# A hybrid decoder layer: the up projection of seven chunks by Strassen's seven block products

## The chip, the cores and the metric

The kernel runs on one core of one Trainium2 chip. The metric is the device time of one execution in microseconds, median of several runs. TensorE (PE) multiplies, VectorE (DVE) and ScalarE (ACT) do elementwise work, GpSimd (POOL) little, and SyncE (SP) issues the DMAs. Each engine works through its own queue in order; semaphores tie the queues together.

## The reference

One decoder layer over 256 tokens of width 2048, all in float32:

```python
h = rmsnorm(x, mix_pre_gain)
q_a, k_a, v_a, q_r, f_r, i_r, g_r = split(h @ w_in)          # w_in: 2048 x 5376
m = concat[rmsnorm(sliding_window_attention(q_a, k_a, v_a, sinks)), hgrn2(q_r, f_r, i_r, g_r)]
x = x + rmsnorm(m @ w_out, mix_post_gain)                     # w_out: 2048 x 2048
h = rmsnorm(x, mlp_pre_gain)
u = relu(h @ w_up)                                            # w_up: 2048 x 8192
x = x + rmsnorm((u * u) @ w_down, mlp_post_gain)              # w_down: 8192 x 2048
```

Most of the arithmetic lies in the two projections of the last block, `w_up` and `w_down`.

## The kernel before

**Numbers.** Every operand of a large product is split in two float32r parts: `hi`, the value cast by ACT (line 84 for weights), and `lo`, the value less `hi`, by DVE (line 85). A product is three matmuls, hi x hi, hi x lo and lo x hi (`three`, lines 103 to 107).

**Two forms of product.** The *token-major* form (`wide_step`) holds 128 tokens of the activations in PE and streams 512 weight columns; its result has tokens on the partitions. The *feature-major* form (`feature_step`, lines 113 to 120) holds 128 weight columns and streams the activations: `hi` and `lo` of 256 tokens side by side, 512 columns, against the weight's `hi`, and 256 columns against its `lo`. The two halves of the result stand in one PSUM bank, and `unit_sum` adds them: ACT copies one half, DVE adds the other (lines 140 and 141). A unit (`unit_feature`) is 256 output features: two banks of 16 steps each. Its result has features on the partitions, as the down projection needs it.

**Phases.** First the normalised `x` is transposed, and `w_in` is applied: keys and values, four units for attention (`attention`), and for each of four pairs of recurrent heads two units and one token-major pair (`rnn_pair`). Then `w_out`, token-major, in four column groups of 512. Then the feed-forward part, in four chunks of 2048 features of `w_up`. The first chunk begins with 512 features token-major (they can start while the second 128 tokens are still being normalised); everything else of `w_up` is done in feature-major units, 30 of them. A unit's result is scaled, clipped and squared (`up_evac`), split in `hi` and `lo`, and written to a tile `uT`. After each chunk's up projection stand its 16 down tile rows: four column groups `c` of 512, for each 16 steps on both token blocks. Column groups 0 to 2 are added into `y` by DVE after every chunk; group 3 stays in two PSUM banks to the end.

**Buffers and order.** Weights pass through one pool `wpool` that lives for the whole kernel: three raw tiles of 128x2048 (one megabyte in HBM each), four `hi` and four `lo`. PSUM has three banks named `pj`, three `sc`, one `o`, one `tr`. The order on PE is written out by hand from the last `w_out` group to the first feature unit; everywhere else, and for the other engines and SP throughout, a scheduler sets it from the program's dependences when the kernel is built. A DMA waits in SP's queue until its buffer is free, and so do all DMAs behind it.

**Names and lines** that the change touches: `load_raw`, `split_weight`, `load_unit`, `load_wide`, `load_pair` (70 to 101), `feature_step` and `unit_feature` (113 to 135), `unit_sum` (137), the evacuations in `attention` and `rnn_pair`, the residual and its transposes (`residual` 612, `turn` 619, which writes the transposed `hi` and `lo` in lines 625 and 631), `early_turn` and `up_evac` (662 to 680), and the chunk loop (753 to 773). `mu0` to `mu3`, `hT0` to `hT3` are tags of tiles for activations.

## Time and profile before

| | us |
|---|---|
| median of 3 runs | 1134.54 |
| lowest, highest | 1132.27, 1135.0 |
| profiled execution | 1136.72 |
| its span, first to last instruction | 1134.7 |
| PE busy | 1113.9 |
| DVE busy | 642.8 |
| ACT busy | 554.4 |
| chain of work that ended last, share of PE | 95% |
| bytes read from HBM, mean rate | 201.36 MB, 179 GB/s |

The phases in the span: `w_in` and the heads to 346 us, `w_out` from 321 (its first products lie among the last of the heads) to 414, the feed-forward part from 414 to 1125, the last normalisation to the end. Busy time of PE counts overlapping matmuls once, and the ends of matmuls are modelled; how long one occupies PE is read from the distance between the starts of two. A line "A <- B: total, times, longest" in the list of waits says how long A's engine stood idle until B released it.

### The profile page before, as it was taken

What the parts mean: (1) busy time and instruction counts of PE and PEld (TensorE: products, weight loads), DVE (VectorE), ACT (ScalarE), POOL (GpSimd) and SP (SyncE); (2) the same over time, 40 slices, a digit from 0 to 9 for tenths busy, and PEclk for the clock granted to TensorE, in tenths of its full rate; (3) what the DMA queues carried; (4) which work ended last, traced back from release to release, by engine and by line L of the source; (5) the groups of instructions that cost most, each with busy time, mean ns of one, the idle gap of its engine ahead of it and who ended that gap; (6) DMA issues with size and microseconds to landing.
All of it is one profiled execution on the core that took longest, in us unless ns stands there. A gap on an engine that the chain in (4) does not pass through costs nothing.

```text
span 1134.7 us, 14265 instructions
## 1 busy us (share of the span) xinstructions
PE 1113.9 (98%) x5822; PEld 945.9 (83%) x5822; DVE 642.8 (57%) x728; ACT 554.4 (49%) x747; POOL 25.6 (2%) x56
## 2 busy tenths in 40 slices
PE   8998999999999999999999999999999999999996
PEld 7887788888888888888888888888888888888885
DVE  6755577666655585564445555444655544465453
ACT  6655656645554466553444544334554334454441
POOL 2100001000000010000000000000000000000001
PEclk9999999999999999999999999999999999999998
DMA  8753244444457655746565565555555555655542
GB/s 270 234 165 112 75 148 149 149 148 151 147 196 280 202 197 163 223 162 209 194 198 185 165 211 197 185 189 183 190 182 203 203 188 170 201 177 196 194 139 74
DMA packets 155251, 204.38 MB, mean 180 GB/s; under 512 B 3833, under 2 KB 110898, under 8 KB 154674
## 3 DMA queue, kind: packets, MB, share of 16 engines
q1 hardware_dynamic: 155186, 203.48, 55.0%
q8 instruction: 45, 0.74, 0.3%
q14 instruction: 20, 0.16, 0.0%
HBM read 201.36 MB, written 2.10 MB: 179 GB/s over the span
## 4 chain that ended last, share of the span: by engine, by line
PE 95%; DVE 2%; ACT 0%; issue 0%; POOL 0%; DVEq 0%; ACTq 0%; POOLq 0%
PE pj L118 18%; PE sc L118 10%; PE pj L105 8%; PE pj L106 8%; PE pj L107 8%; PE pj L117 8%; PE sc L107 5%; PE sc L106 5%; PE sc L105 5%; PE sc L117 5%; PE tr L106 1%; PE o L106 1%; PE tr L107 1%; PE o L105 1%; PE tr L105 1%; PE o L107 1%
## 5 line engine op out<-in xcount | busy, mean ns | idle before, releaser
L85 DVE TENSOR_TENSOR wlo<-raw,whi 128x2048 fp32r<-128x2048 f32 (+2 forms) x204 | 427.7, 2102 | 358.2 <-ACT whi L84 357.8
L84 ACT CAST whi<-raw 128x2048 fp32r<-128x2048 f32 (+2 forms) x204 | 357.6, 1760 | 310.7 <-PE sc L107 87.0
L118 PE MATMUL pj<-hT,whi 128*128 128x512 f32 x864 | 309.6, 402 | 3.6 <-DVE qT L141 2.2
L117 PE MATMUL pj<-hT,wlo 128*128 128x256 f32 x810 | 229.7, 284 | 0.4 <-DVE wlo L85 0.3
L118 PEld LDWEIGHTS pj<-hT,whi 128*128 128x128 f32 x864 | 161.7, 190 | 38.3 <-DVE qT L141 2.7
L118 PE MATMUL sc<-hT,whi 128*128 128x512 f32 x480 | 170.0, 398 | 0.0
L117 PEld LDWEIGHTS pj<-hT,wlo 128*128 128x128 f32 x810 | 154.3, 191 | 3.9 <-DVE wlo L85 1.0
L117 PE MATMUL sc<-hT,wlo 128*128 128x256 f32 x450 | 126.6, 281 | 0.0
L118 PEld LDWEIGHTS sc<-hT,whi 128*128 128x128 f32 x480 | 89.3, 188 | 19.7
L105 PE MATMUL pj<-whi,mu 128*128 128x512 f32 x256 | 100.1, 392 | 0.4 <-DVE mg L607 0.4
L106 PE MATMUL pj<-wlo,mu 128*128 128x512 f32 x256 | 99.8, 390 | 0.0
L105 PE MATMUL sc<-whi,mu 128*128 128x512 f32 x256 | 99.6, 389 | 0.0
L106 PE MATMUL sc<-wlo,mu 128*128 128x512 f32 x256 | 99.6, 389 | 0.0
L107 PE MATMUL sc<-whi,mu 128*128 128x512 f32 x256 | 99.6, 389 | 0.0
L107 PE MATMUL pj<-whi,mu 128*128 128x512 f32 x256 | 99.5, 391 | 0.0
L117 PEld LDWEIGHTS sc<-hT,wlo 128*128 128x128 f32 x450 | 85.1, 189 | 1.2
L105 PE MATMUL pj<-whi,hT 128*128 128x512 f32 x160 | 63.9, 402 | 1.1 <-DVE zq L141 1.0
L106 PE MATMUL pj<-wlo,hT 128*128 128x512 f32 x160 | 63.9, 400 | 0.0
L107 PE MATMUL pj<-whi,hT 128*128 128x512 f32 x160 | 63.7, 399 | 0.0
L105 PEld LDWEIGHTS pj<-whi,mu 128*128 128x128 f32 x256 | 48.1, 188 | 10.5 <-DVE mg L607 0.8
L107 PEld LDWEIGHTS pj<-whi,mu 128*128 128x128 f32 x256 | 48.1, 188 | 10.0
L106 PEld LDWEIGHTS sc<-wlo,mu 128*128 128x128 f32 x256 | 48.0, 188 | 10.0
(248 smaller groups left out, 1224.5 us busy)
## 6 DMA issues: line engine op xcount, KB each, us to landing
raw<-in_w_up_dram SPq DMA_DIRECT2D x64, 1024.0 KB, 5.4
raw<-in_w_down_dram SPq DMA_DIRECT2D x64, 1024.0 KB, 5.0
raw<-in_w_in_dram SPq DMA_DIRECT2D x24, 1024.0 KB, 5.4
raw<-in_w_in_dram SPq DMA_DIRECT2D x35, 512.0 KB, 4.1
raw<-in_w_out_dram SPq DMA_DIRECT2D x16, 1024.0 KB, 5.0
xb<-in_x_dram SPq DMA_DIRECT2D x8, 256.0 KB, 6.3
x<-in_x_dram SPq DMA_DIRECT2D x2, 1024.0 KB, 10.5
out_dram<-x SPq DMA_DIRECT2D x6, 256.0 KB, 2.6
```

The costliest lines, as they stand in the source:

```text
L84: nc.scalar.copy(out=hi[:, k], in_=raw[:, k])
L85: nc.vector.tensor_tensor(out=lo[:, k], in0=raw[:, k], in1=hi[:, k].bitcast(F32), op=ALU.subtract)
L105: nc.tensor.matmul(o, lhsT=ah, rhs=bh, start=first, stop=False)
L106: nc.tensor.matmul(o, lhsT=ah, rhs=bl, start=False, stop=False)
L107: nc.tensor.matmul(o, lhsT=al, rhs=bh, start=False, stop=last)
L117: nc.tensor.matmul(ps[:, 0:S], lhsT=al, rhs=both[:, 0, :], start=False, stop=False)
L118: nc.tensor.matmul(ps, lhsT=ah, rhs=both, start=kt == 0, stop=kt == NKT - 1)
```

## The change

The up projection of the last 7168 features is made of seven chunks of 1024. Each chunk is a 256 x 2048 by 2048 x 1024 product, cut in 2 x 2 blocks: tokens in two halves of 128, the depth in two halves of 1024, the features in two halves of 512. Strassen's scheme makes the four result blocks from seven block products instead of eight, at the price of sums of blocks. All products are token-major, three matmuls for each of eight depth steps; a product is made in two halves of 12 matmuls.

- The sums of activation blocks are made once, before the first of the seven chunks, and kept as `hi` and `lo` (`a11`, `s1` to `s4`, `a12`, `a22`). For them `turn` writes the transposed activations a third time, in float32 (`hf`).
- The sums of weight blocks are made by DVE in place for each chunk, on the raw tiles `X`, `P`, `Q` (`add`), between the splits: 8 additions of 128x2048, and 14 splits instead of 8.
- The result blocks are made by accumulating products in PSUM where the signs allow, otherwise by DVE with intermediate results in `scr` and in the unused quarter of `y`. Because they are token-major, every 128x512 block is transposed on PE (`turn_u`) before the down projection, four turns for each chunk; the turns of a chunk stand among the next chunk's first products.
- The chunk loop interleaves: after every product of chunk `ch` stands one half (4 depth steps on both token blocks) of a down tile of chunk `ch - 1`. The order on PE is written out by hand to the end.
- The first 1024 features are done token-major without Strassen's scheme.
- In the first phase a feature unit now makes three 256-wide matmuls for each step into one half of a single bank, so that `unit_sum` goes away: one DVE operation scales and evacuates the unit. The query is scaled there, and the distance penalty of attention no longer passes through ACT.
- The weight pool is entered three times instead of once: `wpool_a` to the end of the heads, `wpool_b` to the start of the chunks, `wpool_c` behind that, with three `hi`, three `lo` and two each of `X`, `P`, `Q` and `d` (down weights). The residual `x2` is written to HBM and read again at the end.

The diff, cut to its core:

```diff
-    wpool = ctx.enter_context(tc.tile_pool(name="wpool", bufs=4))
+    pool_w = tc.tile_pool(name="wpool_a", bufs=4, side="right")
+    wp = [pool_w.__enter__()]
...
     def feature_step(ps, ch, hT, ct, kt):
...
+        three(ps[:, ct * 256:(ct + 1) * 256], [t[:, kt % 8, ct * P:(ct + 1) * P] for t in ch[kt // 8]],
+              [hT[kt // 4][:, kt % 4, i, :] for i in range(2)], kt == 0, kt == NKT - 1)
...
-        qT = unit_sum(apool, "t2", ps_q, 3, "qT")
+        qT = apool.tile([P, 2, S], F32, tag="t2", name=nm("qT"), bufs=3)
+        nc.vector.tensor_tensor(out=qT, in0=ps_q, in1=rb, op=ALU.mult)
...
     pa.__exit__(None, None, None)
-    bpool = ctx.enter_context(tc.tile_pool(name="phase_b", bufs=1))
+    pool_w.__exit__(None, None, None)
+    keep = ctx.enter_context(tc.tile_pool(name="keep", bufs=1, side="right", reuse_waits="tile"))
+    upool = ctx.enter_context(tc.tile_pool(name="upool", bufs=1, side="right", reuse_waits="tile"))
+    pool_w = tc.tile_pool(name="wpool_b", bufs=4, side="right", reuse_waits="tile")
+    wp[0] = pool_w.__enter__()
+    pb = tc.tile_pool(name="phase_b", bufs=1, reuse_waits="tile")
...
+        nc.sync.dma_start(out=x2_dram[tb], in_=x2[tb])
+        hf[tb] = keep.tile([P, NKT, P], F32, tag=f"acc{tb}", name=nm("hf"))
...
+        for i in range(4):
+            kt = 4 * c + i
+            nc.scalar.activation(out=hf[tb][:, kt, :], in_=ps[:, i * P:(i + 1) * P], func=AF.Copy,
+                                 scale=g_mlp[:, kt:kt + 1])
...
+    def turn_u(uT, cb, tb, u, tag, bufs):
+        tp = bank(tag, bufs)
         for i in range(4):
+            nc.tensor.transpose(tp[:, i * P:(i + 1) * P], u[:, i * P:(i + 1) * P], ident)
+        u2 = upool.tile([P, 4, P], F32, tag="u2", name=nm("u2"), bufs=2)
         nc.scalar.activation(out=u2, in_=tp.rearrange("p (a t) -> p a t", a=4), func=AF.Square)
+        hi, lo = (uT[cb][:, :, i, tb * P:(tb + 1) * P] for i in range(2))
         nc.scalar.copy(out=hi, in_=u2)
         nc.vector.tensor_tensor(out=lo, in0=u2, in1=hi.bitcast(F32), op=ALU.subtract)
...
+    nc.vector.tensor_sub(out=tmp, in0=hn[1, 0], in1=hn[1, 1])
+    a11 = split_act(hn[0, 0], "ex")
+    s1 = split_act(tmp, "mu2")
...
+    def product(o, aT, w, h, fresh):
+        for j in range(4):
+            kt = 4 * h + j
+            (ah, al), (bh, bl) = (aT[:, kt, 0, :], aT[:, kt, 1, :]), (w[0][:, j, :], w[1][:, j, :])
+            for i, (a, b) in enumerate(((ah, bh), (ah, bl), (al, bh))):
+                nc.tensor.matmul(o, lhsT=a, rhs=b, start=fresh and kt == 0 and i == 0, stop=kt == 7 and i == 2,
+                                 skip_group_check=not fresh)
...
+    for ch in range(1, NCH):
...
+        for h in range(2):
+            if ch > 1 or h == 1:
+                next_turn()
+            X.append(raw_tile("X", w_up_v, 4 * h, f0))
+            product(bank_a, a11, split_weight(None, X[h], bufs=3), h, True)
+        nc.scalar.copy(out=sv, in_=bank_a)
+        for h in range(2):
+            next_turn()
+            Pq.append(raw_tile("P", w_up_v, 4 * h, f0 + 512))
+            add(X[h], Pq[h])
+            product(bank_b, s1, split_weight(None, X[h], bufs=3), h, True)
+        nc.scalar.copy(out=m5, in_=bank_b)
...
+        down(d, 0, 0, uT)
+        for h in range(2):
+            Q.append(raw_tile("Q", w_up_v, 8 + 4 * h, f0 + 512))
+            add(X[h], Q[h])
+            product(bank_a, s2, split_weight(None, X[h], bufs=3), h, False)
+        nc.scalar.copy(out=um, in_=bank_a)
+        down(d, 0, 1, uT)
...
+        for h in range(2):
+            add(Pq[h], Q[h])
+            product(bank_a, s3, split_weight(None, Pq[h], bufs=3), h, False)
+        nc.vector.tensor_sub(out=u[1, 1], in0=m5, in1=bank_a)
+        relu(u[1, 1], u[1, 1])
+        down(d, 1, 0, uT)
+        for h in range(2):
+            product(bank_b, s4, split_weight(None, Q[h], bufs=3), h, False)
...
+        down(d, 1, 1, uT)
+        for h in range(2):
+            R.append(raw_tile("P", w_up_v, 8 + 4 * h, f0))
+            add(X[h], R[h])
+            product(bank_a, a22, split_weight(None, X[h], bufs=3), h, False)
+        relu(u[0, 1], bank_a)
+        down(d, 2, 0, uT)
+        for h in range(2):
+            product(bank_c, a12, split_weight(None, R[h], bufs=3), h, True)
...
+        down(d, 2, 1, uT)
+        down(d, 3, 0, uT)
...
+        down(d, 3, 1, uT)
```

Line numbers from here on in rows of the changed kernel are its own: 86 is the weight's `lo` (85 before), 85 its `hi` (84), 767 an `add`, 672 and 671 the turned tile's `lo` and `hi`, 797 the addition into `y`.

**SP at the joint between the heads and `w_out`.** Before; `raw` from `in_w_in_dram` are the last head pair's weights, `gmix` is the gain behind `w_out`, `x_0` and `x_1` the residual's input:

```order
L99 DMA raw_2879<-in_w_in_dram 128x4x256 x2
L74 DMA raw_3041<-in_w_out_dram 128x4x512
L74 DMA raw_3047<-in_w_out_dram 128x4x512
L74 DMA raw_3053<-in_w_out_dram 128x4x512
L74 DMA raw_3059<-in_w_out_dram 128x4x512
L74 DMA raw_3169<-in_w_out_dram 128x4x512
L74 DMA raw_3175<-in_w_out_dram 128x4x512
L74 DMA raw_3181<-in_w_out_dram 128x4x512
L74 DMA raw_3187<-in_w_out_dram 128x4x512
L74 DMA raw_3297<-in_w_out_dram 128x4x512
L74 DMA raw_3303<-in_w_out_dram 128x4x512
L579 DMA gmix<-in_mix_post_gain_dram 128x2048
```

After:

```order
L100 DMA raw_3175<-in_w_in_dram 128x4x256 x2
L572 DMA gmix<-in_mix_post_gain_dram 128x2048
L576 DMA x_0_3335<-in_x_dram 128x2048
L576 DMA x_1_3336<-in_x_dram 128x2048
L75 DMA raw_3351<-in_w_out_dram 128x4x512
L75 DMA raw_3357<-in_w_out_dram 128x4x512
L75 DMA raw_3363<-in_w_out_dram 128x4x512
```

The ten loads of `w_out` that stood ahead of `gmix` and `x` now stand behind them.

**DVE at the start of a feed-forward chunk.** Before, two units of the second chunk (`z` and `u` are evacuations of the unit before, `mu` is `uT`):

```order
L141 TENSOR_TENSOR z_5081<-pj_5048,z_5081 128x256
L675 SCALAR_TENSOR_TENSOR u_5086<-z_5081,rb_mlp 128x512
L85 TENSOR_TENSOR wlo_5190<-raw_5187,whi_5189 128x2048
L680 TENSOR_TENSOR mu_4910<-u_5088,mu_4910 128x2x256
L141 TENSOR_TENSOR z_5170<-sc_5104,z_5170 128x256
L85 TENSOR_TENSOR wlo_5273<-raw_5270,whi_5272 128x2048
L141 TENSOR_TENSOR z_5170<-sc_5137,z_5170 128x256
L675 SCALAR_TENSOR_TENSOR u_5175<-z_5170,rb_mlp 128x512
L85 TENSOR_TENSOR wlo_5279<-raw_5276,whi_5278 128x2048
L680 TENSOR_TENSOR mu_4911<-u_5177,mu_4911 128x2x256
```

After, the third Strassen chunk. These are the last 12 of 16 rows that begin with the chunk's first split; the four ahead of them are the splits of the two `X` tiles, the first `add` to `X`, and one to `P`:

```order
L767 TENSOR_TENSOR X_5518<-X_5518,P_5574 128x2048
L86 TENSOR_TENSOR wlo_5550<-X_5491,whi_5549 128x2048
L672 TENSOR_TENSOR uT_5478<-u_5487,uT_5478 128x4x128
L767 TENSOR_TENSOR P_5574<-P_5574,Q_5645 128x2048
L86 TENSOR_TENSOR wlo_5578<-X_5518,whi_5577 128x2048
L767 TENSOR_TENSOR X_5491<-X_5491,Q_5626 128x2048
L672 TENSOR_TENSOR uT_5478<-u_5514,uT_5478 128x4x128
L86 TENSOR_TENSOR wlo_5597<-d_5594,whi_5596 128x2048
L672 TENSOR_TENSOR uT_5477<-u_5542,uT_5477 128x4x128
L767 TENSOR_TENSOR X_5518<-X_5518,Q_5645 128x2048
L86 TENSOR_TENSOR wlo_5630<-X_5491,whi_5629 128x2048
L672 TENSOR_TENSOR uT_5477<-u_5570,uT_5477 128x4x128
```

Between two splits stood one small evacuation; now additions of whole weight tiles stand there, and the four rows of `uT`, which the next down tile reads, lie between them.

**ACT at the same place.** After, with the squares of the turned blocks (`u` from `sc`, line 669), their casts (671), and the casts of weights (85):

```order
L85 CAST whi_5577<-X_5518 128x2048
L671 CAST uT_5478<-u_5514 128x4x128
L849 COPY scr<-pj_5479 128x512
L85 CAST whi_5596<-d_5594 128x2048
L669 ACTIVATE u_5542<-sc_5537 128x512
L671 CAST uT_5477<-u_5542 128x4x128
L85 CAST whi_5629<-X_5491 128x2048
L855 COPY scr<-pj_5480 128x512
L669 ACTIVATE u_5570<-sc_5565 128x512
L671 CAST uT_5477<-u_5570 128x4x128
```

Before:

```order
L140 COPY z_5081<-pj_5015 128x256
L84 CAST whi_5183<-raw_5181 128x2048
L140 COPY z_5081<-pj_5048 128x256
L84 CAST whi_5189<-raw_5187 128x2048
L677 ACTIVATE u_5088<-u_5086 128x512
L679 CAST mu_4910<-u_5088 128x2x256
```

The last turned block's square and cast stand behind the cast of an `X` tile whose second addition is one of the DVE rows above; before, an evacuation's square stood behind a cast of a raw tile.

More of the change, by code (lines that the diff above doesn't have):

```diff
@@ L70, in load_raw @@
     def load_raw(src, pieces=1):
-        raw = wpool.tile(list(src.shape), F32, tag="raw", name=nm("raw"), bufs=3)
+        raw = wp[0].tile(list(src.shape), F32, tag="raw", name=nm("raw"), bufs=3)
         n = src.shape[1] // pieces
@@ L75, in load_raw, with split_weight @@
         return raw
-    def split_weight(src, raw=None, pieces=1):
+    def split_weight(src, raw=None, pieces=1, bufs=4):
         raw = load_raw(src) if raw is None else raw
-        hi = wpool.tile(list(raw.shape), F32R, tag="whi", name=nm("whi"), bufs=4)
-        lo = wpool.tile(list(raw.shape), F32R, tag="wlo", name=nm("wlo"), bufs=4)
+        hi = wp[0].tile(list(raw.shape), F32R, tag="whi", name=nm("whi"), bufs=bufs)
+        lo = wp[0].tile(list(raw.shape), F32R, tag="wlo", name=nm("wlo"), bufs=bufs)
         n = raw.shape[1] // pieces
@@ L650, in tile_hybrid_layer, with new_u @@
             evac_post(c, tb, banks[tb])
[L654 to L663 removed]
+    order_pe = tc.manual_schedule(engines={mybir.EngineType.PE})
+    order_pe.__enter__()
+    def new_u():
+        return upool.tile([P, 512], F32, tag="u", name=nm("u"), bufs=4)
@@ L712, in tile_hybrid_layer, with new_uT @@
-    rb2 = got["rb"]
-    up_evac(ps_up2, 2)
-    gpost2 = bpool.tile([P, D], F32, tag="gpost", name="gmlp")
-    nc.sync.dma_start(out=gpost2, in_=mlp_post.broadcast_to([P, D]))
-    y = [bpool.tile([P, D], F32, tag=f"acc{i}", name=nm("y")) for i in range(2)]
+    def new_uT(first="mu0", second="mu1"):
+        return [hpool.tile([P, 4, 2, S], F32R, tag=t, name=nm("uT")) for t in (first, second)]
+    ch = load_wide(w_out_v, 0, 3 * 512, pieces=2)
+    banks = [bank("pj"), bank("pj")]
+    for kt in range(NKT):
+        wide_step(banks[0], ch, mixT, 0, kt)
@@ new lines, in tile_hybrid_layer @@
+    evac_post(3, 0, banks[0])
+    residual(0)
+    for kt in range(NKT):
+        if kt in (6, 8, 10, 12):
+            turn(0, kt // 2 - 3)
+        wide_step(banks[1], ch, mixT, 1, kt)
+    evac_post(3, 1, banks[1])
+    residual(1)
+    uT = new_uT()
+    up_w = load_wide(w_up_v, 0, 0, pieces=2)
+    norm2(0)
+    ps = [bank("pj"), bank("pj")]
+    for kt in range(NKT):
+        if kt in (8, 10, 12, 14):
+            turn(1, kt // 2 - 4)
+        wide_step(ps[0], up_w, h2T, 0, kt)
+    u = [new_u(), new_u()]
@@ new lines, in tile_hybrid_layer @@
+    relu(u[0], ps[0], rh[:, 0:1])
+    norm2(1)
+    for kt in range(NKT):
+        if kt == 4:
+            turn_u(uT, 0, 0, u[0], "tr", 1)
+        wide_step(ps[1], up_w, h2T, 1, kt)
+    relu(u[1], ps[1], rh[:, 1:2])
+    up_w = load_wide(w_up_v, 0, 512)
+    ps = [bank("pj"), bank("pj")]
+    for i in range(4):
+        for tb in range(2):
+            if i == 1 and tb == 0:
+                turn_u(uT, 0, 1, u[1], "tr", 1)
+            if i == 1 and tb == 1:
+                rb2 = spread(rh, "rb_mlp")[:, 0, :]
+            for j in range(4):
+                wide_step(ps[tb], up_w, h2T, tb, 4 * i + j)
@@ new lines, in tile_hybrid_layer, with down_weight, down_half @@
+    down_banks = {}
+    def down_weight(ch, c, h):
+        return split_weight(None, raw_tile("d", w_down_v, 8 * ch + 4 * h, c * 512), bufs=3)
+    def down_half(ch, c, h, uT, w, tbs=(0, 1)):
+        if c == 3 and not held:
+            held.extend([bank("o", 1), bank("tr", 1)])
+        if h == 0 and 0 in tbs:
+            down_banks[c] = held if c == 3 else [bank("sc"), bank("sc")]
+        banks = down_banks[c]
+        for tb in tbs:
+            for j in range(4):
+                kt = 4 * h + j
+                first = kt == 0 and (c < 3 or ch == 0)
+                last = kt == 7 and (c < 3 or ch == NCH - 1)
+                three(banks[tb], tok(uT, kt, tb), (w[0][:, j, :], w[1][:, j, :]), first, last)
+            if h == 1:
+                evac_down(ch, c, tb, banks[tb])
@@ new lines, in tile_hybrid_layer @@
+    tail["x2"] = []
+    for tb in range(2):
+        t = wp[0].tile([P, D], F32, tag="X", name=nm("x2"), bufs=2)
+        nc.sync.dma_start(out=t, in_=x2_dram[tb])
+        tail["x2"].append(t)
+    tail["g"] = wp[0].tile([P, D], F32, tag="P", name="gmlp", bufs=2)
+    nc.sync.dma_start(out=tail["g"], in_=mlp_post.broadcast_to([P, D]))
+    ch = NCH - 1
+    for c in range(3):
+        for h in range(2):
+            down(ch, c, h, uT)
+    w = [down_weight(ch, 3, h) for h in range(2)]
+    for tb in range(2):
+        for h in range(2):
+            down_half(ch, 3, h, uT, w[h], (tb,))
```

233 lines of the change are left out of this document (108 added, 125 removed).

## The prediction

> **What bounds the kernel now.** I read the page's busy shares and chain first, then busy time by stretches, the pieces of the chain in time, the groups by form, and last the DMA queue.
>
> ```profile
> PE 1113.9 (98%) x5822; PEld 945.9 (83%) x5822; DVE 642.8 (57%) x728; ACT 554.4 (49%) x747; POOL 25.6 (2%) x56
> PE 95%; DVE 2%; ACT 0%; issue 0%; POOL 0%; DVEq 0%; ACTq 0%; POOLq 0%
> ```
>
> TensorE (PE) is busy for 98% of the span and carries 95% of the chain that ended last. VectorE (DVE) and ScalarE (ACT) have 40% and 50% of free time, but averaged over everything. The stretches (columns: us, busy us and count of PE, PEld, DVE, ACT, POOL, then granted clock, DMA share, GB/s) tell more:
>
> ```profile
> 14.00:24.00 10.00, 9.03 (x74) 8.51 (x72) 7.35 (x15) 7.05 (x15) 0.00 (x0) 1.00 1.00 312
> 86.00:96.00 10.00, 8.54 (x45) 7.29 (x44) 4.38 (x14) 5.17 (x17) 0.00 (x0) 0.83 0.33 105
> 139.00:146.00 7.00, 6.02 (x15) 4.56 (x16) 4.75 (x12) 5.93 (x13) 0.00 (x0) 0.53 0.00 0
> 404.00:430.00 26.00, 26.00 (x134) 21.59 (x133) 22.65 (x49) 22.92 (x61) 2.20 (x4) 1.00 0.63 203
> 470.00:1125.00 655.00, 655.00 (x3277) 554.87 (x3276) 340.13 (x260) 282.71 (x248) 2.10 (x3) 1.00 0.56 184
> ```
>
> From 470 to 1125 us PE never waits and runs at full clock. Two things stand out elsewhere: between 404 and 430 us ACT is nearly full too (22.92 of 26 us), and in two early stretches where PE has short waits its clock is cut.
>
> **Matmuls.** The pieces of the chain give the true spacing, since listed matmul times overlap:
>
> ```profile
> 500.61 0.46 PE pj L118 x2
> 598.95 0.46 PE sc L118 x2
> 610.24 0.46 PE pj L118 x2
> 605.17 0.12 PE pj L117
> 605.29 0.23 PE pj L118
> 429.52 0.44 PE tr L665 x4
> ```
>
> The first three are middles of feature units. One unit of 32 steps takes 610.24 - 598.95 = 11.29 us. Between the first two lie one unit and a down projection tile row of 384 matmuls: (98.34 - 11.29) / 384 = 0.2267 us for each of 512 columns. A 256-wide one takes 0.12, a turn of four transposes 0.44.
>
> Removed: 30 feature units of the up projection, 338.7 us. Added: seven chunks of seven products of 24 matmuls and a second plain block of 96, 1272 x 0.2267 = 288.4. **Products: -50.3.** Every token-major tile must be turned: 32 turns instead of 2, 30 x 0.44, **+13.2.** The 12 units left in the first phase use three 256-wide matmuls for a step: 384 x (0.36 - 0.353), **+2.7.** The order of PE shows 12 matmuls for each half product, so the saving is real.
>
> ```profile
> L118 PE MATMUL pj<-hT,whi 128*128 128x512 f32 x864 | 309.6, 402 | 3.6 <-DVE qT L141 2.2 <-DVE f L141 0.9 <-ACT whi L84 0.4
> PE pj L118 <- DVE qT L141: 2.2, 2, 1.3
> PE sc L391 <- ACT p L383: 1.4, 2, 1.2
> PE pj L105 <- DVE zq L141: 1.0, 1, 1.0
> ```
>
> A unit now fills one PSUM bank instead of two and leaves in one operation, so the first phase's waits for the two-step sum (2.2 + 0.9 + 1.0) may go, with the clock cuts that follow (0.17 x 10 us in the window at 86). I take **-6**, between 0 and -11. Without any new wait the profiled execution, 1136.7 us (span 1134.7), becomes 1096.3.
>
> **New waits at the joints.** The weight pool is now left and entered anew, and the first load of `w_out` stands behind three others in SP's queue.
>
> ```profile
> 326.46 18.45 SPq L74 DMA_DIRECT2D raw<-in_w_out_dram  x4
> 346.21 0.35 SPq L579 DMA_DIRECT2D gmix<-in_mix_post_gain_dram  x1
> 346.61 0.90 SPq L582 DMA_DIRECT2D x<-in_x_dram  x2
> x<-in_x_dram SPq DMA_DIRECT2D x2, 1024.0 KB, 10.5
> raw<-in_w_up_dram SPq DMA_DIRECT2D x64, 1024.0 KB, 5.4
> ```
>
> Before, four `w_out` loads went out up to 20 us ahead of the gain and `x`, under the last head pair's projections. Now all four wait until that pair's readout has freed the memory, when PE has nothing left. Four megabytes at the peak of 312 GB/s are 13.4 us, the cast 1.9 and the subtraction 2.3 (rows below), the last partly beside products: 17. The pair's own readout, beside `w_out` products until now, is bare too; its longest wait is this row of the list of waits:
>
> ```profile
> DVE on L557 <- POOL r L168: 7.5, 4, 3.1
> ```
>
> That is 3 more: **+20**. Bounds: a lone load of 5.4 plus the cast, 7.3; behind the 10.5 of `x` 19.7, with the readout 22.8.
>
> ```profile
> L84 ACT CAST whi<-raw 128x2048 fp32r<-128x2048 f32 x172 | 328.9, 1912 | 292.6 <-PE sc L107 87.0 <-PE pj L118 62.0 <-PE pj L107 56.0
> L85 DVE TENSOR_TENSOR wlo<-raw,whi 128x2048 fp32r<-128x2048 f32 x172 | 394.0, 2290 | 342.9 <-ACT whi L84 342.5
> L85 DVE TENSOR_TENSOR wlo<-raw,whi 128x1024 fp32r<-128x1024 f32 x24 | 28.4, 1221 | 10.2 <-ACT whi L84 10.0
> L625 ACT ACTIVATE hT<-sc,vcol 128x128 fp32r<-128x128 f32 x32 | 9.1, 378 | 2.6 <-PE sc L622 2.6
> L680 DVE TENSOR_TENSOR mu<-u,mu 128x512 fp32r<-128x512 f32 x30 | 20.6, 686 | 0.0
> L744 DVE TENSOR_TENSOR y<-sc,y 128x512 f32<-128x512 f32 x12 | 8.3, 688 | 3.6 <-PE sc L107 3.6
> L427 DVE TENSOR_SCALAR o_attn<-o_attn,r 128x1024 f32<-128x1024 f32 x2 | 1.4, 747 | 0.0
> ```
>
> The transposed activations are copied once more in plain float32: 32 copies like those of line 625, 12.1 us on ACT in the stretch where it has 3 us free, holding the banks that PE's transposes need. **+12**, the upper end because ACT works in order; the lower is 0.
>
> Before the first Strassen product DVE runs 15 operations of 1024 elements on the activations, all ahead of the first weight split: 15 x 1.22 + 2.29 = 20.6 us from the moment the row scale is there, while PE has five groups of 12 matmuls, 13.6. That is 7.0. From there to the first down tile stand eight large rows and a small one (19.0) against 12.2 of PE: 6.8. The next split comes 7.6 after that against 5.4: 2.2. With the load wait below, **+18**, from 9 (the activations' splits partly done early) to 22 (two casts on the path).
>
> **New waits in the loop.** A chunk costs DVE 22 splits, 8 adds and 13 small operations: 30 x 2.29 + 13 x 0.69 = 77.7 us, against PE's 360 x 0.2267 + 1.8 = 83.4. It fits on the whole, but not in place. From the split of the chunk's first tile to the fourth turned tile's low part, which the first down tile needs for its third matmul, DVE has 16 rows in its order: 12 large, 4 small, 27.5 + 2.7 = 30.2 us. PE has there only two product pairs, four turns and two matmuls: 48 x 0.2267 + 1.8 + 0.45 = 13.1. DVE can start early only when a weight buffer is free. There are three, so the first one comes free two down tiles (48 matmuls, 10.9 us) ahead; a split and two evacuations stand before it (3.7), leaving 7.2. Wait: 30.2 - 7.2 - 13.1 = 9.9. Later an add stands 3.7 us behind the split that lets its load go, and the load takes 5.4: 1.6 more. That is 11.5 a chunk, and in the rest PE has 70.7 us of matmuls against DVE's 47.4, so nothing more. Six chunks, the second to the seventh: **+69**. Bounds: full head start and no load wait, 6.2 a chunk (37); none, 18.7 (112).
>
> Costed at nothing: the loads, because a chunk's 16.8 MB in about 95 us are 177 GB/s, below the 184 of the stretch from 470 us (the two writes and reads of `x2` add 4 MB in all); and ACT, with 22 casts of 1.91 and 15 small operations of 0.6, 51 us of a chunk's 95. If a load came late, its add would hold all of DVE behind it, as in the 1.6 above.
>
> No float32 add of 128x2048 is in the trace. By line 427, a one-input operation, it would take 1.49 us; by line 85, with two inputs and the same shape, 2.29, which I take as the nearer row. The Trainium skill (VectorE: DVE Perf Modes, the perf-mode tier table) gives 2293 ns for a two-input float32 operation of that size, as it cannot use the faster mode of one-input operations; by its price the sum stays, by line 427 it would be 29 us less. No run here shows the add yet.
>
> **Clock.** In the windows at 86 and 139 waits of at most 1.3 us were followed by cuts worth 0.17 x 10 = 1.7 and 0.47 x 7 = 3.3 us. Longer waits, one group in each of seven chunks and one at the first joint: 8 x 2, **+16**, between 0 and 8 x 3.3 = 27. The Trainium skill (TensorE: Matmul & The Clock Gate, Part 1) has the clock halved only after an idle window of about 3.4 us. By that rule the chunks' waits, which come in pieces, could all stay under the threshold, this term would be 0 and the forecast 1213; the trace does not bear it out, since its cuts followed waits of 1.3 us at most.
>
> Sum: 1096.3 + 20 + 12 + 18 + 69 + 16 = 1231.3. The median of the runs, 1134.5, lies 2.2 below the profiled execution, so I forecast **1229 us**. Its own range goes from 1155 to 1270; all terms at their ends together would reach further.
>
> **Rivals.** *DVE covers the chunk* (not slower). If the add goes at line 427's rate, six adds save 4.8 us of the 30.2, and with a full head start the wait is 6.2 - 4.8 = 1.4 a chunk. The entry's waits shrink likewise, loads come early, the clock stays. Then 1096.3 + 20 + 12 + 7 x 1.4 = 1138, or 1136 by the median; with the joints at their lower ends of 7.3 and 0, 1111. It decides near an add of 1.5 us and a start 10.9 us ahead. For it: DVE's total is below PE's. Against it: line 85. Chance 0.09.
>
> *Waits of the foreseen kind at half size*: chunk waits of 6.2 and a full clock, joints near their lower ends: 1096.3 + 10 + 6 + 10 + 37 = 1159, or 1140 to 1165. Chance 0.07.
>
> *No head start*: the rings of three hold DVE back through every down tile, 18.7 a chunk: 6 x 7.2 = 43 more, 1269. For it: the same buffers are what DVE waits for while PE stands. Chance 0.08.
>
> The forecast keeps 0.76. Left out of 1155 to 1270 are the first rival, about half of the second and of the third: 0.17. A measurement of this kernel can tell about 0.3% from no change. Faster comes from the first rival alone (0.06), within 0.3% from it too (0.03), slower is the rest (0.91).
>
> **What would show it.** Right: PE waits of 6 us and more in each chunk, released by DVE's `uT` row and by ACT's `uT` cast; some 15 us of idle PE before the first `w_out` product with its release from a cast; DVE rows of the adds near 2.29 us; granted clock below 1 inside the loop. Wrong: adds near 1.5 us, PE at 100% between the chunks, or `w_out` landing early. If PE's busy time does not fall by some 35 us, the product count is wrong.

## The result and the profile after

The changed kernel takes **1221.2 us** (median of 4 runs, 1219.9 to 1224.9), the kernel before 1134.8 (1132.3 to 1137.6): ratio 1.077, 95% interval 1.073 to 1.080. It is slower by 86 us. The prediction said 1229, between 1155 and 1270. The profiled execution took 1224.9 us, with a span of 1223.0.

First the page of the changed kernel: the busy shares, then the chain that ended last.

```profile
PE 1132.5 (93%) x5678; PEld 938.1 (77%) x5678; DVE 855.0 (70%) x776; ACT 639.3 (52%) x779; POOL 22.8 (2%) x56
...
PE 77%; DVE 11%; DMA 4%; issue 4%; ACT 3%; SPq 0%; POOL 0%; DVEq 0%; ACTq 0%; POOLq 0%
```

PE's share of the chain fell from 95% to 77%, and the largest part of what took its place is DVE with 11%. No engine is full, so waits were added. But PE's busy time rose, from 1113.9 to 1132.5 us, though it has fewer columns to multiply. Waits alone do not do that. The list of PE's waits names the places (us in total, times, longest):

```profile
PE sc L108 <- DVE uT L672: 24.5, 6, 5.1
PE sc L106 <- ACT uT L671: 14.9, 5, 3.0
PE pj L106 <- ACT whi L85: 11.4, 1, 11.4
PE pj L763 <- DVE wlo L86: 6.0, 5, 2.2
PE pj L763 <- ACT whi L85: 4.5, 1, 4.5
PE sc L107 <- DVE wlo L86: 3.7, 2, 3.5
PE tr L546 <- DVE on L541: 3.5, 1, 3.5
PE sc L619 <- ACT hf L632: 3.2, 2, 2.7
```

The first stands in all six chunks from the second on and the second in five of them, where the first down tile needs the turned tiles `uT`. The third and the seventh are the joint to `w_out`. Of the 14.2 us of the next three, 9.5 lie at the entry to the first chunk, and the last is the copy `hf`. By stretches (columns as in the prediction: us, busy us and count of each engine, granted clock, DMA share, GB/s), these are the joint, the turns of the activations, the entry, and a chunk:

```profile
320.00:341.00 21.00, 4.56 (x21) 2.77 (x21) 4.17 (x6) 6.05 (x12) 1.20 (x2) 0.62 0.77 296
...
425.00:455.00 30.00, 26.77 (x119) 21.28 (x119) 22.20 (x49) 29.47 (x91) 2.28 (x6) 0.89 0.62 211
455.00:520.00 65.00, 55.15 (x221) 43.14 (x220) 54.84 (x35) 36.09 (x35) 0.00 (x0) 0.89 0.46 162
706.00:802.00 96.00, 88.56 (x376) 70.34 (x376) 75.80 (x44) 50.13 (x37) 0.00 (x0) 0.96 0.51 175
```

In a chunk of about 96 us DVE is busy for 75.8 and PE for 88.6: both have free time, in different places. In time order (start us, length, engine, line, tiles, and in brackets the idle time before) a chunk's wait looks like this, from the chunk's first turn on:

```profile
781.07 0.60 PE L667 MATMUL sc<-ident,u 128*128 128x128 f32 x4
...
794.06 0.40 PE L763 MATMUL pj<-whi,a 128*128 128x512 f32 x1
797.45 0.51 PE L106 MATMUL sc<-whi,uT 128*128 128x512 f32 x1 [2.99 <-ACT uT L671]
797.79 0.39 PE L107 MATMUL sc<-wlo,uT 128*128 128x512 f32 x1
802.24 0.80 PE L108 MATMUL sc<-whi,uT 128*128 128x512 f32 x1 [4.06 <-DVE uT L672]
802.83 0.63 PE L106 MATMUL sc<-whi,uT 128*128 128x512 f32 x1
803.25 0.63 PE L107 MATMUL sc<-wlo,uT 128*128 128x512 f32 x1
...
807.48 0.40 PE L107 MATMUL sc<-wlo,uT 128*128 128x512 f32 x1
807.72 0.40 PE L108 MATMUL sc<-whi,uT 128*128 128x512 f32 x1
807.95 0.39 PE L106 MATMUL sc<-whi,uT 128*128 128x512 f32 x1
```

Two things are to be seen. After 7.05 us of waiting the matmuls start 0.43 us apart until about 806.2, half the rate: the clock is cut, and that costs another 1.9 us. And at full clock they start 0.2333 us apart, not 0.2267 as before. The prediction had named the first; the second is new.

On DVE the 16 rows that the prediction counted, from the split of the chunk's first tile to the fourth `uT` row, run from 772.93 to 802.19 without a break. The first two and the last two:

```profile
772.93 2.28 DVE L86 TENSOR_TENSOR wlo<-X,whi 128x2048 fp32r<-128x2048 f32 x1
775.25 2.29 DVE L767 TENSOR_TENSOR X<-X,P 128x2048 f32<-128x2048 f32 x1
...
799.29 2.28 DVE L86 TENSOR_TENSOR wlo<-X,whi 128x2048 fp32r<-128x2048 f32 x1
801.50 0.69 DVE L672 TENSOR_TENSOR uT<-u,uT 128x512 fp32r<-128x512 f32 x1
```

### The profile page after: what moved, and what is told of

It is laid out like the page before. It is cut to its first block, busy times and chain, and to the rows that moved or that the text cites. A ratio compares the mean times of both kernels' runs of the same rounds, so it can differ in the third digit from the quotient of the medians.

```text
span 1223.0 us, 14075 instructions
## 1 busy us (share of the span) xinstructions
PE 1132.5 (93%) x5678; PEld 938.1 (77%) x5678; DVE 855.0 (70%) x776; ACT 639.3 (52%) x779; POOL 22.8 (2%) x56
## 4 chain that ended last, share of the span: by engine, by line
PE 77%; DVE 11%; DMA 4%; issue 4%; ACT 3%; SPq 0%; POOL 0%; DVEq 0%; ACTq 0%; POOLq 0%
PE pj L763 15%; PE pj L107 10%; PE pj L106 9%; PE pj L108 9%; PE sc L108 7%; PE sc L107 7%; PE sc L106 7%; DVE wlo L86 6%; DVE X L767 2%; DMA P<-in_w_up_dram 2%; ACT whi L85 1%; DMA raw<-in_w_in_dram 1%; DVE uT L672 1%; PE tr L107 1%; PE o L107 1%
## 5 line engine op out<-in xcount | busy, mean ns | idle before, releaser
L763 PE MATMUL pj<-whi,a 128*128 128x512 f32 x784 | 259.8, 400 | 4.5 <-ACT whi L85 4.5
L86 DVE TENSOR_TENSOR wlo<-d,whi 128x2048 fp32r<-128x2048 f32 x64 | 146.6, 2291 | 115.7 <-ACT whi L85 115.7
L86 DVE TENSOR_TENSOR wlo<-raw,whi 128x2048 fp32r<-128x2048 f32 (+2 forms) x84 | 152.8, 1832 | 87.2 <-ACT whi L85 87.1
L108 PE MATMUL sc<-whi,uT 128*128 128x512 f32 x384 | 158.7, 413 | 24.5 <-DVE uT L672 24.5
L763 PEld LDWEIGHTS pj<-whi,a 128*128 128x128 f32 x784 | 148.2, 189 | 39.7 <-ACT whi L85 4.9
L85 ACT CAST whi<-raw 128x2048 fp32r<-128x2048 f32 (+2 forms) x84 | 128.1, 1546 | 87.9 <-PE pj L108 38.5
L106 PE MATMUL sc<-whi,uT 128*128 128x512 f32 x384 | 158.2, 412 | 14.9 <-ACT uT L671 14.9
L107 PE MATMUL sc<-wlo,uT 128*128 128x512 f32 x384 | 158.9, 414 | 4.0 <-DVE wlo L86 3.7
L763 PE MATMUL pj<-wlo,a 128*128 128x512 f32 x392 | 156.8, 400 | 6.0 <-DVE wlo L86 6.0
L85 ACT CAST whi<-X 128x2048 fp32r<-128x2048 f32 x56 | 106.8, 1909 | 93.6 <-DVE X L767 39.9
L108 PEld LDWEIGHTS sc<-whi,uT 128*128 128x128 f32 x384 | 76.0, 198 | 45.6 <-DVE uT L672 27.6
L107 PE MATMUL pj<-hT,whi 128*128 128x256 f32 x384 | 110.6, 288 | 0.0
L106 PE MATMUL pj<-hT,whi 128*128 128x256 f32 x384 | 109.7, 286 | 0.4 <-DVE zq L426 0.4
L106 PEld LDWEIGHTS sc<-whi,uT 128*128 128x128 f32 x384 | 76.2, 199 | 35.6 <-ACT uT L671 17.1
```

The costliest lines, as they stand in the source:

```text
L85: nc.scalar.copy(out=hi[:, k], in_=raw[:, k])
L86: nc.vector.tensor_tensor(out=lo[:, k], in0=raw[:, k], in1=hi[:, k].bitcast(F32), op=ALU.subtract)
L106: nc.tensor.matmul(o, lhsT=ah, rhs=bh, start=first, stop=False)
L107: nc.tensor.matmul(o, lhsT=ah, rhs=bl, start=False, stop=False)
L108: nc.tensor.matmul(o, lhsT=al, rhs=bh, start=False, stop=last)
L763: nc.tensor.matmul(o, lhsT=a, rhs=b, start=fresh and kt == 0 and i == 0, stop=kt == 7 and i == 2, skip_group_check=not fresh)
```

## Experiments

Line numbers in rows of an experiment are those of its own kernel. The changed kernel stands at 1221.2 us and the kernel before at 1135 throughout; ratios are to the kernel before. "Chunk" below is the time from one chunk's first turn to the next one's, read from rows like those under e7: 95.6 us in the changed kernel from its third chunk to its fourth, and 96.2 on the mean of its five such stretches (95.6 to 97.6).

**The joint (e1).** The pools that outlive the first phase go to the left, and the weight pool is not left and entered anew.

```diff
-    pool_w.__exit__(None, None, None)
-    keep = ctx.enter_context(tc.tile_pool(name="keep", bufs=1, side="right", reuse_waits="tile"))
-    upool = ctx.enter_context(tc.tile_pool(name="upool", bufs=1, side="right", reuse_waits="tile"))
-    pool_w = tc.tile_pool(name="wpool_b", bufs=4, side="right", reuse_waits="tile")
-    wp[0] = pool_w.__enter__()
+    keep = ctx.enter_context(tc.tile_pool(name="keep", bufs=1, reuse_waits="tile"))
+    upool = ctx.enter_context(tc.tile_pool(name="upool", bufs=1, reuse_waits="tile"))
```

> The changed kernel, but the pools that outlive phase A lie on the left side, where phase A's tiles were, and one weight pool serves phases A and B. Theory: the first w_out splits waited because the new weight pool took over memory of earlier tiles and its loads stood behind two others in SP's queue. Then PE's 11.4 us wait for ACT whi at 338.66 and its neighbours (17.2 us from 319 to 341) shrink below 4, the granted clock of that stretch (0.63) returns to about 1, and the time falls by 15 to 25 us, to 1196-1206. Rival: the raw ring would hold the loads back anyway; then under 6 us are won. The chunk loop stays as it is (about 95.7 us a chunk).

Measured: 1202.4 us, ratio 1.059 (1.057 to 1.061), 18.8 less. In this kernel's stretches PE never waits there:

```profile
300.00:341.00 41.00, 41.00 (x224) 33.68 (x223) 24.16 (x31) 20.59 (x32) 1.51 (x2) 1.00 0.46 155
```

In SP's queue nine loads of `w_out` stand ahead of `gmix` and `x` again. So the joint is a matter of memory and of the order in that queue, as forecast (the edit changes both at once); the price forecast was 20.

**Additions on GpSimd (e2), and none (e3).** Both ask whether DVE's amount of work ahead of the turned tiles makes the chunk's wait.

```diff
-    def add(t, v):
-        nc.vector.tensor_add(out=t, in0=t, in1=v)
+    def add(t, v, eng=nc.vector):
+        eng.tensor_add(out=t, in0=t, in1=v)
...
-            add(X[h], Q[h])
+            add(X[h], Q[h], nc.gpsimd)
-            add(Pq[h], Q[h])
+            add(Pq[h], Q[h], nc.gpsimd)
-            add(X[h], R[h])
+            add(X[h], R[h], nc.gpsimd)
```

> The changed kernel, but six of a chunk's eight weight additions (X+Q, P+Q, X+R) on GpSimd instead of VectorE. Theory (DVE's backlog ahead of the turned tiles' low parts makes the chunk's wait): the waits at the first down tile (24.5 + 14.9 us in all) fall under 10, the granted clock of the loop rises from 0.96 to 0.99 or more, a chunk takes 87 to 89 us instead of 95.7, the time falls by 45 to 55 us, to 1166-1176. Rival A (what holds the first down tile is the turns' own path: square and cast on ACT behind other casts): some 3 us a chunk remain for ACT's uT and only 20 to 28 us are won. Rival B (an addition on GpSimd takes about 5.1 us by its 128x512 row of 1.27, and its chain of X becomes the bound): PE waits for ACT whi out of X, and the chunk stays at 93 us or more.

Measured: 1297.3 us, ratio 1.143 (1.141 to 1.145). The theory's figure missed by far. The wait at the turned tiles did fall, from 24.5 to 3.9 us, but PE waits 58.2 and 37.2 us for `wlo` instead. The groups by form show why (busy us, mean ns):

```profile
L86 DVE TENSOR_TENSOR wlo<-d,whi 128x2048 fp32r<-128x2048 f32 x64 | 204.8, 3200 | 110.3 <-ACT whi L85 110.3
...
L767 POOL TENSOR_TENSOR P<-P,Q 128x2048 f32<-128x2048 f32 x14 | 85.9, 6137 | 283.4 <-DVE X L767 178.5 <-ACT whi L85 88.3 <-issue 16.6
...
L86 DVE TENSOR_TENSOR wlo<-Q,whi 128x2048 fp32r<-128x2048 f32 x14 | 62.5, 4464 | 0.0
L767 DVE TENSOR_TENSOR X<-X,P 128x2048 f32<-128x2048 f32 x14 | 53.5, 3827 | 0.4
```

DVE's own rows, 2.29 us in every other kernel here, take 3.20, 3.83 and 4.46 on the mean of these groups while GpSimd adds, and GpSimd takes up to 6.14 (its spans are rough) instead of the 5.1 I had estimated. The Trainium skill (SBUF — State Buffer, Summary: rules for kernel authors) says that a DVE operation with two SBUF inputs and a GpSimd operation that reads SBUF block each other; the trace agrees in kind, with the numbers above, and I had not reckoned with it. The run says nothing on the rivals, only that this engine is no help here.

```diff
     def add(t, v):
-        nc.vector.tensor_add(out=t, in0=t, in1=v)
+        pass
```

> The changed kernel with all eight weight additions of each chunk left out (the products use the unadded tiles; the same loads, splits and matmuls remain). Theory: the additions' 8 x 2.29 us of DVE a chunk are what makes its wait; a chunk takes 86 to 89 us, the clock in the loop is 0.99 or more, and the time falls by 48 to 60 us, to 1162-1174. Rival: the wait comes from the place of the turns in the order (PE has nothing between them and the first down tile); then 3 us a chunk remain and the time stays above 1185.

Measured, in a single run: 1162.7 us, in the theory's range. The wait at the turned tiles is down to 6.3 us in six places, the clock is full in the loop, a chunk takes 87.45 us. So DVE's additions make most of the wait. Whether it is their number or their place, this run can't tell.

**The first phase alone (e4).** The kernel before, with three 256-wide matmuls for a feature step into one bank, in the units of `w_in` alone; a unit is read by one multiplication by the row scale, and the distance penalty no longer passes through ACT, as the change does it.

```diff
+    def unit_narrow(wv, c0, hT, pieces=1):
...
+                nc.tensor.matmul(o, lhsT=ah, rhs=bh, start=kt == 0, stop=False)
+                nc.tensor.matmul(o, lhsT=ah, rhs=bl, start=False, stop=False)
+                nc.tensor.matmul(o, lhsT=al, rhs=bh, start=False, stop=kt == NKT - 1)
...
-        ps_q = unit_feature(w_in_v, 1280 + 256 * p, hT)
-        zq = unit_sum(apool, "k2", ps_q, 3, "zq")
-        nc.vector.tensor_tensor(out=zq, in0=zq, in1=rb, op=ALU.mult)
+        ps_q = unit_narrow(w_in_v, 1280 + 256 * p, hT)
+        zq = apool.tile([P, 2, S], F32, tag="k2", name=nm("zq"), bufs=3)
+        nc.vector.tensor_tensor(out=zq, in0=ps_q, in1=rb, op=ALU.mult)
```

> The kernel before, with the first phase's part of the change alone: feature products 256 wide into one bank, evacuated by one operation. By the prediction's terms -6 (from -11 to 0) for the waits and +2.7 for the added steps: about -3 us, ratio 0.997 (0.993 to 1.002). Rival: twice the weight loads per column cost more than one bank saves, ratio 1.003 or more. Its down projection is that of the kernel before, so its matmul spacing there (0.227 us before, 0.233 in the changed kernel) says whether that difference belongs to the chip or to the kernel.

Measured: 1131.8 us, ratio 0.9971 (0.9959 to 0.9982), 3.2 less. In its down projection 383 matmuls from 678.65 to 765.46 us are 0.2267 apart. The same chip gave 0.2333 in e3: the difference belongs to the kernel.

**Where the weights lie (e5, e6).** The `w_out` loop is the same code in both kernels, yet its spacing differs. What differs is the address. In the kernel before the weight tiles begin at multiples of 128 bytes. The change counts them from the right end of the memory, and there they begin 96 bytes behind such a multiple (one lies at 139232 in the built program).

```diff
+    ctx.enter_context(tc.tile_pool(name="pad", bufs=1, side="right")).tile([P, 24], F32, name="pad")
     pool_w = tc.tile_pool(name="wpool_a", bufs=4, side="right")
```

> The changed kernel with 96 unused bytes per partition at the right end of SBUF, so that every pool on that side begins at a multiple of 128 bytes instead of 96 behind one. Theory: the weight tiles, which the 512-wide matmuls read as their moving operand, lie across 64-byte borders since the change put them on the right, and that makes 0.2333 us between matmuls out of 0.2267 (33 pieces instead of 32 of a 2048-byte row). Then their spacing is 0.2267 again, and 3,672 such matmuls (1,176 of products, 1,536 down, 576 of w_out and the first w_up tiles, 384 in phase A) save up to 24.6 us: 1197 to 1203 us. Rival: the spacing comes from the greater load of DVE and ACT on the same memory; then it stays at 0.2333 and the time within 3 us of 1221.

Four matmuls of the `w_out` loop, first in the changed kernel, then in e5:

```profile
349.93 0.39 PE L106 MATMUL pj<-whi,mu 128*128 128x512 f32 x1
350.16 0.39 PE L107 MATMUL pj<-wlo,mu 128*128 128x512 f32 x1
350.39 0.40 PE L108 MATMUL pj<-whi,mu 128*128 128x512 f32 x1
350.63 0.39 PE L106 MATMUL pj<-whi,mu 128*128 128x512 f32 x1
```

```profile
349.68 0.39 PE L107 MATMUL pj<-whi,mu 128*128 128x512 f32 x1
349.91 0.39 PE L108 MATMUL pj<-wlo,mu 128*128 128x512 f32 x1
350.13 0.39 PE L109 MATMUL pj<-whi,mu 128*128 128x512 f32 x1
350.36 0.39 PE L107 MATMUL pj<-whi,mu 128*128 128x512 f32 x1
```

Three steps take 0.70 us in the first and 0.68 in the second: 0.2333 and 0.2267. The spacing is as the theory says, but the time is 1211.6 (ratio 1.068, 1.066 to 1.070), 9.7 less and not 20. A chunk's matmuls now need some 2.2 us less, but the mean of the same five stretches falls only from 96.2 to 95.6. The rest went into more waiting (39.9 us listed in the five, 37.1 before) and into more time at the halved clock. The five stretches as one, in the changed kernel and then in e5:

```profile
589.30:1070.52 481.22, 443.92 (x1882) 352.35 (x1881) 376.92 (x216) 250.62 (x185) 0.00 (x0) 0.96 0.51 175
```

```profile
582.88:1060.99 478.11, 438.10 (x1882) 354.94 (x1880) 375.91 (x216) 250.65 (x185) 0.00 (x0) 0.95 0.51 176
```

The opposite edit, on the kernel before:

```diff
+    ctx.enter_context(tc.tile_pool(name="pad", bufs=1)).tile([P, 8], F32, name="pad")
     wpool = ctx.enter_context(tc.tile_pool(name="wpool", bufs=4))
```

> The kernel before with 32 unused bytes ahead of its weight pool, nothing else. Theory of the address: its 2,400 token-major matmuls (1,536 down, 480 of w_out and w_up, 384 in phase A) go from 0.2267 to 0.2333 us, about +16 us, ratio 1.012 to 1.016; its feature matmuls, whose moving operand is the activations, stay. Rival: ratio 0.998 to 1.002.

Measured: 1149.6 us, ratio 1.013 (1.011 to 1.015). Thirty-two unused bytes make the kernel before slower by 14 us.

**Order (e7, e9, e10).** e7 leaves the work as it is and changes only its order. Steps (a half product or a down tile) stand in a list; VectorE and ScalarE, too, run in the order written. In the core, `run(k, 0)` is a step's weight split, `run(k, 1)` the additions placed with it, `run(k, 3)` its evacuation:

```diff
+    for k in range(len(steps)):
+        steps[k][2]()
+        run(k + AHEAD - 1, 1)
...
+        run(k + AHEAD, 0)
...
+            run(k, 3)
...
+            add_product("a11", ch, "X", "a11", "a", True, post_a11, extra=([], [XP[0]]))
+            add_down((d - 1, 2, 1) if ch == 2 else (d - 1, 3, 0), extra=[XP[1]])
+            add_product("s1", ch, "X", "s1", "b", True, post_s1, extra=([], [XQ[0]]), turns=([T(d, 0, 0)], [T(d, 0, 1)]))
+            add_down((d - 1, 3, 1), extra=[XQ[1]])
+            add_product("s2", ch, "X", "s2", "a", False, post_s2, extra=([], [PQ[0]]),
+                        turns=([T(d, 1, 0)], [T(d, 1, 1)]))
+            add_down((d, 0, 0), extra=[PQ[1]])
```

`AHEAD` is 3. The rest of the chunk alternates as before; the second column tile after the last chunk also gets banks of its own.

> The changed kernel with the same work in another order: the down projection's last column tile goes between the next chunk's first products, the turned tiles come one by one ahead of half products, VectorE and ScalarE run in a written order (split of three steps ahead, additions early, evacuations behind it), and the first chunk starts on two down tiles while the activations are prepared. Theory: DVE's 75 us a chunk fit under PE's 87, and only the place of the 16 rows ahead of the first down tile made the wait. Then PE's idle time in a chunk falls from 7.05 us to 2.5 or less, its clock cut of about 1.9 us goes with it, the entry loses 5 to 10 us, and the time falls by 45 to 60 us, to 1161-1176. Rival: DVE's amount of work is the bound; then the waits only move to other tiles and less than 15 us are won (1206 or more).

Measured: 1153.0 us, ratio 1.016 (1.014 to 1.018), 68 less, more than expected. A stretch in the loop, then the first turns of two chunks in succession:

```profile
706.00:802.00 96.00, 96.00 (x421) 77.41 (x421) 84.58 (x51) 55.83 (x41) 0.00 (x0) 1.00 0.58 196
```

```profile
666.76 0.60 PE L667 MATMUL sc<-ident,u 128*128 128x128 f32 x4
752.50 0.60 PE L667 MATMUL sc<-ident,u 128*128 128x128 f32 x4
```

PE does not wait at all, the clock is full, and a chunk takes 85.74 us, with every addition in it and DVE busy for 84.58 of 96. So the rows' place made the wait, not their number: DVE can carry this work. Of the 68 us, 52.5 lie in the five stretches from one chunk's first turn to the next; the rest is the last chunk and the entry, which the edit reorders too. The two halves of the edit in the chunk were also run alone; the new order at the entry is in neither. e9 has PE's order alone:

```diff
+        if ch > 1:
+            down(ch - 2, 3, 0, uT)
...
+        if ch > 1:
+            down(ch - 2, 3, 1, uT)
+            uT = new_uT()
+            while turns:
+                next_turn()
...
-        down(d, 0, 0, uT)
+        if ch == 1:
+            down(d, 0, 0, uT)
...
+        if ch > 1:
+            down(d, 0, 0, uT)
```

> The changed kernel with one half of e7: PE's order alone (the last column tile of the down projection between the next chunk's first products, all four turns behind it), VectorE and ScalarE as the scheduler orders them. Theory (it takes both halves: DVE's rows must also stand in the order in which PE needs them): the wait moves from the turned tiles to the held column tile, and the time stays at 1210 to 1228 us. Rival: PE's order alone does it; 1175 us or less.

Measured: 1214.7 us, ratio 1.071 (1.069 to 1.073). As the theory says, the wait moved to the held column tile, which stands in bank `o`:

```profile
PE o L107 <- DVE wlo L86: 21.8, 10, 2.9
...
PE sc L108 <- DVE uT L672: 10.1, 6, 1.7
```

e10 has e7's written order of the other two engines around PE's old order. (In its first chunk the first half of the second product takes its tile before the addition; the amount of work is the same.)

```diff
+            add_product("a11", ch, "X", "a11", "a", True, post_a11, extra=([], [XP[0]]),
+                        turns=([T(d, 1, 1)], [T(d, 1, 0)]))
+            add_product("s1", ch, "X", "s1", "b", True, post_s1, extra=([XP[1]], [XQ[0]]),
+                        turns=([T(d, 0, 1)], [T(d, 0, 0)]))
+        add_down((d, 0, 0), extra=[XQ[1]])
```

> The other half of e7: the written order of VectorE and ScalarE (splits three steps ahead, additions early, evacuations behind), with PE's order in the chunk as the changed kernel has it. Theory: with two products ahead of the first down tile DVE still has its 16 rows against 13 us of PE; the waits at the turned tiles stay at 6 to 8 us a chunk, and 5 to 15 us are won in all: 1205 to 1217. Rival: the written order alone does it; 1175 us or less.

Measured: 1229.2 us, ratio 1.085 (1.082 to 1.087). The waits at the turned tiles stay (28.3 and 15.0 us), as the theory says, but it is 8 us slower instead of 5 to 15 faster: this written order, which was made for another order on PE, is worse here than the scheduler's. One half alone gives -6.5 us, the other +8, both together -68.

**The clock (e11).** Additional matmuls fill the waits.

```diff
-        down(d, 0, 0, uT)
+        if ch > 1:
+            spare[:] = [bank_c]
+            spin(12)
+            down_half(d, 0, 0, uT, down_weight(d, 0, 0), gap=14)
+        else:
+            down(d, 0, 0, uT)
```

> The changed kernel with 26 additional matmuls a chunk (from the second on), whose result is not used, in the two waits at the first down tile: 12 ahead of it, 14 behind its second matmul. Theory A (the halved clock behind the wait costs the chunk about 1.9 us): PE's idle time there falls below 1.5 us, the granted clock of the loop rises from 0.96 to 0.99 or more, and six chunks win 8 to 12 us: 1209 to 1213. Theory B (DVE's rows set the length of a chunk, so that PE's slower matmuls are covered by the next wait): the clock rises all the same, the waits beyond the filling grow, and the time stays within 4 us of 1221.

Measured: 1210.9 us, ratio 1.068 (1.066 to 1.069), 10.3 less: theory A. With 26 useless matmuls a chunk the kernel is faster, since the clock holds:

```profile
706.00:802.00 96.00, 93.97 (x409) 74.76 (x408) 75.31 (x43) 50.09 (x37) 0.00 (x0) 1.00 0.51 175
```

That is 1.7 us for each of the six waits. Theory B, by which DVE's rows alone set a chunk's length, is out.

**Together (e12, e8).** e12 is e7 with the padding of e5.

> e7 and e5 together. With e7's order PE no longer waits in the chunks, so that the 0.0067 us of each of the 3,672 matmuls should count in full: 24.6 us less than e7 (1153), 1126 to 1131, where the padding alone gave 10 (theory: in the changed kernel DVE set the length of a chunk and hid the rest). Rival: it gives 10 us here too, 1143.

Measured: 1136.1 us, ratio 1.000 (0.999 to 1.002): 16.9 less than e7, between theory and rival. The stretch and the chunk that answer to e7's:

```profile
706.00:802.00 96.00, 96.00 (x433) 79.46 (x432) 83.86 (x48) 58.32 (x43) 0.00 (x0) 1.00 0.63 217
```

```profile
660.72 0.60 PE L668 MATMUL sc<-ident,u 128*128 128x128 f32 x4
744.25 0.60 PE L668 MATMUL sc<-ident,u 128*128 128x128 f32 x4
```

PE does 433 instead of 421 matmuls in the same 96 us, and a chunk takes 83.53 us. From the first product to the end, where PE hardly waits, the gain is full: 660.2 us in e7 (490.99 to 1151.2), 643.2 here (489.82 to 1133.0), 17.0 where 2,712 matmuls of 0.0067 make 18.1. Of the 6.4 that the 960 ahead of it could give, 1.2 came out; PE waits at the joint and the entry there, in both kernels.

e8 adds e1 to it, and two edits at the entry:

```diff
-        for i in range(4):
-            kt = 4 * c + i
-            nc.scalar.activation(out=hf[tb][:, kt, :], in_=ps[:, i * P:(i + 1) * P], func=AF.Copy,
-                                 scale=g_mlp[:, kt:kt + 1])
+        nc.vector.tensor_tensor(out=hf[tb][:, 4 * c:4 * c + 4, :], in0=ps.rearrange("p (a t) -> p a t", a=4),
+                                in1=g_mlp[:, 4 * c:4 * c + 4].unsqueeze(2).broadcast_to([P, 4, P]), op=ALU.mult)
...
+        if kt == 10:
+            rb2 = spread(rh, "rb_mlp")[:, 0, :]
...
-            if i == 1 and tb == 1:
-                rb2 = spread(rh, "rb_mlp")[:, 0, :]
```

> All of it together: pools on the left and one weight pool for both phases (e1), 96 bytes of padding (e5), the order of e7, the plain copies of the activations as one DVE operation of 512 elements instead of four ACT operations of 128, and the row scale spread earlier. Theory: the parts are separate causes and add up: 1221 - 19 - 22 - 52 - 8 = 1120, range 1105 to 1130, faster than the kernel before (1135). Rival: they share the same hidden time, and the sum stays above 1135.

Measured: **1109.7 us, ratio 0.978 (0.976 to 0.980)**. This version beats both kernels. The parts add up: 1221.2 - 18.8 (e1) - 68.2 (e7) - 16.9 (e12 against e7) = 1117.3, and the two last edits and what the parts do for one another are the remaining 7.6. Its longest PE wait is 4.0 us, at the entry.

## Why the prediction was right, point by point

The verdict and the mechanism hold. The change saves products and pays with waits, of which most come from DVE's order ahead of the turned tiles. The time was 8 us from the forecast, partly by luck: the waits were sized 45 us too large, and some 30 us of clock and addresses were too little or not there at all. The steps, by the prediction's own terms:

| Term | Forecast, us | Shown, us |
|---|---|---|
| First phase | -6 + 2.7 | -3.2 (e4, the sum alone) |
| PE's work in a chunk | 83.4 | 83.5 (e12), 85.7 as the change places the weights (e7) |
| Joint to `w_out` | +20 | +18.8 (e1); 17.2 of it listed idle time |
| Copies `hf` | +12 | +3.2 listed |
| Entry to the first chunk | +18 | +9.9 listed |
| Chunk waits, six | +69 | +43.6 listed |
| Clock after the waits | +16 | 1.7 a chunk (e11), about 21 in all, an estimate |
| Place of the weights | none | +24.6 by count (e5, e6, e12) |

- **Products and turns: right.** That 83.4 us is what PE needs for a chunk can be seen only in e12, where nothing hides it. The expected gain is real, and e8 shows it.
- **The last sign: badly chosen.** "If PE's busy time does not fall by some 35 us, the product count is wrong": it rose by 18.6, and the count is right all the same. In e8, with the same products, PE is busy for 1082.5 us, 31.4 less than before. In the changed kernel the wider spacing (24.6 us by count) and the cut clock (about 21) outweigh the saving.
- **Rows of the additions: right.** They take 2.29 us as forecast; the rival that needs 1.49 is out. With no addition at all (e3) the kernel is still slower than before.
- **Chunk waits: right in place and cause, too large.** The step that was off is "Wait: 30.2 - 7.2 - 13.1 = 9.9", and the 1.6 for a late load behind it. The trace shows 7.3 us a chunk (43.6 over six). DVE's `uT` row and ACT's `uT` cast release 39.4 of it, as I had said, and the split in the second product the rest. For the chunk shown above the same sum reads 29.3 - 8.1 - 14.1 = 7.1: the 16 rows take 29.3 us, DVE begins them 8.1 us before the chunk's first turn, and PE has 14.1 us of work from that turn to the third matmul of the down tile. Each of the three terms was off by 0.9 to 1.0, and each made the forecast wait longer. What sets DVE's head start was not tried. No wait of PE for `R` is listed.
- **The joint: right.** See e1.
- **The copies and the entry: right in kind, too large.** `hf` was taken at its upper end, "because ACT works in order", and the lower end was nearer: PE is busy for 26.77 of 30 us there. At the entry DVE's 15 operations and the first split take 20.3 us (474.92 to 495.21) against the 20.6 forecast. PE waits 6.0 us ahead of the first product (forecast 7.0) and 3.9 up to the first down tile (6.8); the 2.2 at the next split and the wait for a load do not show.
- **The clock: the size was right.** The prediction took 2 us for each of eight places, and e11 measures 1.7 for each of six. The four others, at the joint, the copies and the entry, are an estimate: with e11's filling PE still works for 20.6 us at the halved clock there, and half of that is 10.3; both together make the 21. The prediction's reason was weaker: it said that cuts followed waits of 1.3 us at most, but those windows held two short waits each (0.57 and 0.89 us before 90.93). The Trainium skill's rule (TensorE: Matmul & The Clock Gate, Part 1) of a cut after an idle window of some 3.4 us is nearer to this than I allowed: every wait of PE of 2.98 us or more in these runs lies in a stretch at the halved clock or directly ahead of one. It does not explain the shorter waits that were cut (last section). The full clock in the chunks, which the prediction named as possible by that rule, did not come about, since the second pieces of their waits are 3.6 to 5.1 us long.
- **The missing term.** "1272 x 0.2267" carried the spacing of the kernel before over to a kernel whose weights lie elsewhere. That the new pools stand on the right was in the diff, and no row of the kernel before could show its price.

The sum: 1231.3 - 45 (waits sized too large: 119 forecast, 74 listed) + 5 (clock) + 25 (addresses) = 1216, against 1224.9 profiled. Some 9 us are not assigned by any run. Most of them lie in the loop: on the mean a chunk loses 96.2 - 85.7 = 10.5 us against e7, and the listed wait (7.4) and the cut (1.7) make 9.1 of it.

## What to carry to other kernels

When work is moved between engines, write down for the stage the order in which each engine will run it, and not only its sum: here the same rows cost some 10 us a chunk in one order and nothing in another, and of the two halves of the new order one alone won 6.5 us in all and the other lost 8. A gain on one engine counts in full only where that engine does not wait: the same 0.0067 us a matmul gave 10 us beside the waits and 17 without them. And when a matmul's spacing changes between two kernels with the same instructions, look at where its operands lie.
